# The sequential scan of a state-space layer: three operations a step on all groups in place of six on halves

## The chip, the cores and the metric

The kernel runs on one core of a Trainium2 chip. The metric is the device time of one execution in microseconds (us). Before the change it is 1076.48 us, the median of three runs between 1076.04 and 1077.04. One execution was also taken with the hardware profiler; it took 1074.8 us, and its instructions span 1073.0 us.

## The reference

One layer of a hybrid backbone on 1024 latent tokens of width 1024, with 256 context tokens ahead of them. What matters here is the S5 mixer: 64 groups of 16 channels, each with 64 complex states, scanned forwards and backwards.

```python
for d in range(2):                                   # forward, backward
    lb_re, lb_im, da_re, da_im, bb_re, bb_im = _s5_discretize(...)
    cu_re, cu_im = _apply_b(ucg, bb_re, bb_im)       # context tokens
    hc_re, hc_im = _diag_scan(cu_re, cu_im, da_re, da_im, rev)
    lu_re, lu_im = _apply_b(ug, bb_re, bb_im)        # latent tokens
    lu_re = lu_re.at[:, start].add(lb_re * h0_re - lb_im * h0_im)   # start from the context's last state
    lu_im = lu_im.at[:, start].add(lb_re * h0_im + lb_im * h0_re)
    h_re, h_im = _diag_scan(lu_re, lu_im, da_re, da_im, rev)        # h_t = lam_bar * h_(t-1) + bu_t
    y = y + _readout(h_re, h_im, c_re[d], c_im[d])
out = y + d_skip * u;  z = gelu(out);  y = z * sigmoid(z @ glu_w + glu_b)
x = x + g1 * y
x = x + g2 * mlp(modulate(rmsnorm(x)))               # squared ReLU, 1024 -> 4096 -> 1024
return rmsnorm(x)
```

## The kernel before

The state vector lies on the 128 partitions: 64 states forwards, 64 backwards. A column of the state tiles is one (group, real or imaginary part, time slot). Time is cut into chunks: 8 tokens make one local sum, computed by TensorE (`states`), and the recurrence runs over those chunks. It is done as a tree: `ups` (lines 501 to 509, with `step`, lines 468 to 477) combines the chunks pairwise twice, the **scan** (lines 684 to 714) goes through every fourth chunk in order, and `fill_fours` and `fill_pairs` (lines 675 and 737) go back down. What remains is the readout by TensorE, the gate and the MLP, whose large products are done by a seven-product block scheme and in three passes of rounded parts (`mm3`, line 782).

The scan has 39 steps, `q` = 1 to 39. Step `q` reads the state of slot `2q-1` and updates slot `2q+1`. `slot` (line 650) gives a view of 64 groups by 2 parts, 128 columns; its neighbouring columns are 28 words apart in the context tile `CT` and 132 words apart in the latent tile `LT`. The complex product needs four real products per group, and two additions collect them. Before the change, a step is six VectorE operations, two of each kind, on 32 groups each (`hf` = 0, 1):

- line 710 multiplies the 64 columns of a half of the old state, each used twice, by `L32`, the transition over 32 tokens, which lies in PSUM. It writes 128 columns to `m12[hf]` in PSUM (bank 1 for one half, bank 6 for the other).
- line 712 adds one half of these products, with the parts exchanged, to the new slot and writes 64 columns to `m3` in SBUF.
- line 714 adds the other products and `m3` and writes 64 columns to the new slot.

The order of work is written out by hand; every engine runs its own queue in program order, and a reader waits by semaphore for the writer, on the same engine too. Ahead of some steps stand other pieces: the finish of the kernels of a block of groups on VectorE (`k_finish`, lines 582 to 595, ahead of steps 9, 14, 20 and 28, each followed by eight stores on the SP queue), their products and copies on TensorE and ScalarE (steps 1, 6, 12, 20, 31), TensorE's conditioning products with their loads (line 406), two turns of a tile on ScalarE (line 668, at step 35) and, at step 34, a first part of `fill_fours` on GpSimd. After the last step come, on VectorE, `fill_fours` and `fill_pairs` of the first blocks (lines 473 to 476 are the four operations of `step`); GpSimd does those of one block; ScalarE copies each result (`hc_copy`, lines 734 and 735) for TensorE's readout (lines 763 and 764).

Of the kernel before, what the change touches and what calls it, by code (L numbers as in the profile page):

```python
# [10 lines left out]
OP = mybir.AluOpType  # L11
# [36 lines left out]
def kernel(ctx, tc, cst, bc, x, xl, ada_w, glu_w, w1, w2, out):  # L48
    nc = tc.nc
    V, S, P, PE, SP = nc.vector, nc.scalar, nc.gpsimd, nc.tensor, nc.sync  # L50
# [6 lines left out]
    UT = sp.tile([128, 2560], F32, name="UT")  # L57
# [4 lines left out]
    PS = pp.tile([128, 4096], F32, name="PS")  # L62
# [6 lines left out]
    def vw(ap, *dims):  # L69

        if len(dims) == 1:
            return ap
        names = "abcdef"[:len(dims)]
        return ap.rearrange("p (%s) -> p %s" % (" ".join(names), " ".join(names)),
                            **{names[i]: dims[i] for i in range(len(dims))})

    def size(dims):
        n = 1
        for d in dims:
            n *= d  # L80
        return n

    def at(tile_, off, *dims):
        return vw(tile_[:, off:off + size(dims)], *dims)
# [5 lines left out]
    def bank(i, n=512, o=0):  # L90
        return PS[:, 512 * i + o:512 * i + o + n]
# [86 lines left out]
    q = [at(UT, KT + 192 + 64 * i, 64) for i in range(6)]  # L178
# [56 lines left out]

    LR = [PS[:, o:o + 64] for o in (2048, 2240)]
    LI = [vw(PS[:, o + 64:o + 192], 64, 2) for o in (2048, 2240)]
    L32 = vw(PS[:, 2560:2816], 2, 32, 2, 2)
    TA, TB = 2432, 2960
    L32R, L32I = PS[:, 3840:3904], PS[:, 3904:3968]  # L240

# [21 lines left out]
        V.tensor_copy(L32I, pwi[:, :, 10])  # L263

    def scan_transitions():
        l32 = L32.rearrange("p a g k c -> p (a g) k c")
        V.tensor_copy(l32[:, :, 0], L32R[:, :, None].to_broadcast([128, 64, 2]))
        V.tensor_copy(l32[:, :, 1, 0], L32I)
        V.tensor_scalar(l32[:, :, 1, 1], L32I, -1.0, None, op0=OP.mult)
# [124 lines left out]
    def load_aw2(n, eng=SP):  # L394
        if n < 32:
            part, k = 2 + n // 8, n % 8
            eng.dma_start(out=aw2(n), in_=ada_w[128 * k:128 * k + 128, 1024 * part:1024 * part + 1024])

    def cond2_next():
        n = nc2[0]  # L400
        if n == 32:
            return
        nc2[0] += 1
        part, k = 2 + n // 8, n % 8
        for s in range(4):
            PE.matmul(bank(7)[32 * s:32 * s + 1, 0:256], sc[:, k, 0:1], aw2(n)[:, 256 * s:256 * s + 256], start=k == 0, stop=k == 7)
        late.extend([n + 2] if n + 2 <= C2C else [n + 2, n + 3] if n + 2 == C2C + 1 else [n + 3])
        if k < 7:
            return
        rw = sb(KS + 1024 * (part % 2), 1024)[0:1]  # L410
        for s in range(4):
            S.copy(rw[:, 256 * s:256 * s + 256], bank(7)[32 * s:32 * s + 1, 0:256])
        turns.append((part, rw))

    def cond2_turn():
        part, rw = turns.pop(0)
        for j in range(8):
            PE.transpose(bank(0)[:, 8 * part + j:8 * part + j + 1], rw[:, 128 * j:128 * j + 128], ident[0:1, 0:1])
# [60 lines left out]
    def woven(*streams):  # L479

        streams = [list(q) for q in streams]
        n = max(map(len, streams))
        for i in range(n):
            for q in streams:
                if i < len(q):
                    q[i]()
# [74 lines left out]
    def k_blocks(j):  # L561
        bd = sb(BD, 8, 2, 48)
        gs = slice(8 * j, 8 * j + 8)
        for c, b_ in ((0, br), (1, bi)):
            S.copy(bd[0:64, :, c, 32:48], b_[0:64, gs])
            S.copy(bd[64:128, :, c, 0:16], b_[64:128, gs])

    def k_mm(j, hlf):
        g8, bd, b = gt(j), sb(BD, 8, 2, 48), bank((2, 3)[hlf])
        for g in range(4):  # L570
            gg = 4 * hlf + g
            for c in range(2):
                PE.matmul(b[0:48, 128 * g:128 * g + 128], bd[:, gg, c], g8[:, gg, c], start=c == 0, stop=c == 1)  # L573

    def k_evac(j, hlf):
        bv = bank((2, 3)[hlf]).rearrange("p (g h t) -> p g t h", g=4, t=8)
        gh = slice(4 * hlf, 4 * hlf + 4)
        S.copy(ksr(j, 0, 8, 15, 16)[:, gh, 0:8], bv[0:16])
        S.copy(ksr(j, 0, 8, 15, 16)[:, gh, 8:15], bv[32:48, :, 1:8])
        S.copy(ksr(j, 1920, 8, 16)[:, gh], bv[32:48, :, 0])  # L580

    def k_finish(j, eng=V):

        k0, kf, dj = ksr(j, 0, 8, 15, 16)[:, :, 7], ksr(j, 1920, 8, 16), ksr(j, 2048, 8, 16)
        ks = kf
        if eng is V:
            r = 32 + 64 * (j % 2)
            dj, ks = (vw(PS[r:r + 16, o:o + 128], 8, 16) for o in (3200, 3328))
        eng.tensor_tensor(dj, ident[32:48, None, 32:48].to_broadcast([16, 8, 16]),
                        C("dg")[32:48, 8 * j:8 * j + 8, None].to_broadcast([16, 8, 16]), op=OP.mult)  # L590
        eng.tensor_tensor(ks, kf, dj, op=OP.add)
        eng.tensor_tensor(k0, k0, ks, op=OP.add)
        kd = KD[j].rearrange("(h t g c) -> t h g c", h=16, t=8, g=8)
        for t in range(8):
            SP.dma_start(out=kd[t], in_=ksr(j, 0, 8, 240)[:, :, 16 * (7 - t):16 * (7 - t) + 128])
# [48 lines left out]
    make_g(7)  # L644


    m3 = at(UT, 0, 2, 32, 2)
    m12 = [vw(bank(i, 128), 32, 2, 2) for i in (1, 6)]

    def slot(i):  # L650
        return CT[:, :, :, 0, i] if i < 14 else LT[:, :, :, 0, i - 14]
# [9 lines left out]
    def load_m8(j):  # L661
        SP.dma_start(out=at(X0, 1024 * (j % 2), 1024), in_=KD[j].rearrange("(p c) -> p c", p=128))

    def turn_m8(j):
        src = at(X0, 1024 * (j % 2), 8, 8, 16)
        dst = sb(M8 + 1024 * (j % 2), 8, 16, 8)
        if j <= POOL_FILL:
            S.copy(dst, src.rearrange("p g t h -> p g h t"))
        else:
            P.tensor_copy(dst, src.rearrange("p g t h -> p g h t"))  # L670

    def load_g0(k):
        SP.dma_start(out=at(X0, G0R, 2, 256), in_=glu_w.rearrange("(k p) n -> p k n", p=128)[:, k:k + 2, 0:256])

    def fill_fours(j, a=0, b=8, q0=0, q1=32, eng=None):

        eng = eng or (P if j == POOL_FILL else V)
        gs, n = slice(8 * j + a, 8 * j + b), q1 - q0
        x_ = LT[:, gs, :, 0]
        t = [at(GX, 0, b - a, 2, n)] * 2 if eng is P else [at(UT, 512 * i, b - a, 2, n) for i in range(2)]  # L680
        return step(x_[:, :, :, 2 * q0 + 2:2 * q1 + 1:2], x_[:, :, :, 2 * q0 + 1:2 * q1:2], 1, gs, *t, eng)

    scan_transitions()
    for q in range(1, 40):
        if q - 8 in KSTEP[:-1]:
            k_finish(3 + KSTEP.index(q - 8))
        if q in KSTEP:
            j = 3 + KSTEP.index(q)
            k_blocks(j)
            for hlf in range(2):  # L690
                k_mm(j, hlf)
                k_evac(j, hlf)
        if q % 3 == 0:
            cond2_next()
        while late:
            load_aw2(late.pop())
        if turns and q % 3 == 2:
            cond2_turn()
        if q == M8AT:
            turn_m8(0)  # L700
            turn_m8(1)
        if q == PRE + 7:
            woven(fill_fours(0, q1=PRE, eng=P))
        if q == 12:
            for i in range(2):
                load_m8(i)
            load_g0(0)
        for hf in range(2):
            p = slot(2 * q - 1)[:, 32 * hf:32 * hf + 32]
            V.tensor_tensor(m12[hf], p[:, :, None].to_broadcast([128, 32, 2, 2]), L32[:, hf], op=OP.mult)  # L710
        for hf in range(2):
            V.tensor_tensor(m3[:, hf], m12[hf][:, :, 1, ::-1], slot(2 * q + 1)[:, 32 * hf:32 * hf + 32], op=OP.add)
        for hf in range(2):
            V.tensor_tensor(slot(2 * q + 1)[:, 32 * hf:32 * hf + 32], m12[hf][:, :, 0], m3[:, hf], op=OP.add)
    while turns:
        cond2_turn()
    assert nc2[0] == 32
# [714 lines left out]
    for p in range(7, len(L)):  # L1432
        b, i = L[p]
# [80 lines left out]
    for d in range(8):  # L1514
        o = acc[:, d, toks[1]]
        S.activation(o, o, AF.Identity, scale=C("fg")[:, d:d + 1])
    rb = norm_rows(r_, 2, toks[1])
    for d in range(8):
        o = acc[:, d, toks[1]]
# [64 lines left out]
```

## Time and profile before

| | |
|---|---|
| median of the runs | 1076.48 us |
| profiled execution, whole | 1074.8 us |
| its span | 1073.0 us |
| PE busy | 954.5 us, 89% of the span |
| DVE busy | 884.0 us, 82% |
| ACT busy | 552.9 us, 52% |
| POOL busy | 599.7 us, 56% |
| the chain that ended last, by engine | PE 54%, DVE 24%, ACT 8%, issue 5%, POOL 4%, DMA 4% |

PE is TensorE, DVE is VectorE, ACT is ScalarE, POOL is GpSimd and SP is SyncE, which only issues transfers. A busy share over the whole span is an average over stages with different limits. The scan is one stage of about 50 us out of 1073.0, and what a change in it does is read from that stage and from what follows it.

### The profile page before, as it was taken

To read this page: it belongs to the slowest core of one execution; us is meant where nothing else is said; L and a number is where in the kernel's file an instruction comes from. 1 tells how busy PE (TensorE), PEld (TensorE's weight loads), DVE (VectorE), ACT (ScalarE), POOL (GpSimd) and SP (SyncE) were. 2 spreads that over 40 slices of the span, in tenths; PEclk is the share of its full clock that TensorE was granted. 3 is DMA by queue.
4 is the path that set the end of the run, shared out by engine and by line. 5 is a ranking of instruction groups with operands and counts; after the bars stand their busy time and mean duration, and the time that the engine had idled before them with its cause. 6 is when DMAs were issued, how large, how long until landed. Compare 5 with 4: busy or idle time off the path is not lost.

```text
span 1073.0 us, 15268 instructions
## 1 busy us (share of the span) xinstructions
PE 954.5 (89%) x5276; PEld 783.5 (73%) x5276; DVE 884.0 (82%) x1393; ACT 552.9 (52%) x1015; POOL 599.7 (56%) x411
## 2 busy tenths in 40 slices
PE   4788895656999998899999999998999999999995
PEld 4466674446888776588888888886678888888875
DVE  8799998999946776978665656656899999999997
ACT  6367683346973466656565554545444334343413
POOL 2868999735653814264232232324888787878603
PEclk9969797777999988999999999999999999999998
DMA  9514554775778211165545344469363535451204
GB/s 384 216 46 154 186 155 117 194 212 144 227 243 284 66 40 59 49 207 188 184 138 178 126 162 152 138 203 329 121 224 103 194 120 177 133 162 40 79 1 157
DMA packets 104782, 168.85 MB, mean 157 GB/s; under 512 B 7681, under 2 KB 61953, under 8 KB 103425
## 3 DMA queue, kind: packets, MB, share of 16 engines
q1 hardware_dynamic: 100272, 153.20, 43.6%
q10 hardware_dynamic: 4432, 14.68, 4.1%
q8 instruction: 41, 0.67, 0.3%
q14 instruction: 37, 0.29, 0.1%
HBM read 120.40 MB, written 47.45 MB: 156 GB/s over the span
## 4 chain that ended last, share of the span: by engine, by line
PE 54%; DVE 24%; ACT 8%; issue 5%; POOL 4%; DMA 4%; SPq 1%; DVEq 0%; ACTq 0%; POOLq 0%
PE PS L784 15%; PE PS L785 15%; PE PS L783 15%; DVE T L1364 3%; DVE X L476 2%; PE PS L154 2%; DVE X L475 2%; DMA DY<-X 1%; DVE z L934 1%; DVE PS L474 1%; DVE PS L473 1%; DVE W L934 1%; DVE PS L710 1%; PE PS L573 1%; PE PS L495 1%
## 5 line engine op out<-in xcount | busy, mean ns | idle before, releaser
L783 PE MATMUL PS<-z,W 128*128 128x512 f32 (+1 forms) x432 | 168.6, 390 | 2.9 <-DVE T L1184 1.5
L784 PE MATMUL PS<-z,W 128*128 128x512 f32 (+1 forms) x432 | 167.5, 388 | 2.5 <-DVE z L934 2.5
L785 PE MATMUL PS<-z,W 128*128 128x512 f32 (+1 forms) x404 | 156.7, 388 | 1.3 <-POOL W L934 1.2
L1364 DVE SCALAR_TENSOR_TENSOR T<-PS,T 128x512 f32<-128x512 f32 x160 | 112.1, 739 | 2.4 <-PE PS L785 2.2
L783 PEld LDWEIGHTS PS<-z,W 128*128 128x128 f32 x432 | 81.7, 189 | 21.2 <-DVE T L1463 2.2
L784 PE MATMUL PS<-W 128*128 128x512 f32 (+1 forms) x244 | 93.9, 385 | 3.4 <-DVE W L934 3.2
L784 PEld LDWEIGHTS PS<-z,W 128*128 128x128 f32 x432 | 81.7, 189 | 19.8 <-DVE z L934 3.7
L783 PE MATMUL PS<-W 128*128 128x512 f32 (+1 forms) x244 | 93.3, 382 | 0.0
L785 PEld LDWEIGHTS PS<-z,W 128*128 128x128 f32 x404 | 76.3, 189 | 17.9 <-POOL W L934 2.1
L934 DVE TENSOR_TENSOR z<-z 128x512 fp32r<-128x512 f32 x60 | 81.2, 1378 | 6.0 <-ACT z L937 6.0
L785 PE MATMUL PS<-W 128*128 128x512 f32 (+1 forms) x216 | 82.7, 383 | 1.5 <-POOL W L934 1.5
L785 PE MATMUL PS<-z,A 128*128 128x512 f32 x208 | 81.3, 391 | 2.5 <-POOL A L934 2.5
L934 DVE TENSOR_TENSOR W<-W 128x512 fp32r<-128x512 f32 x49 | 74.2, 1537 | 7.2 <-ACT W L937 7.2
L1212 POOL TENSOR_TENSOR T<-T 128x512 f32<-128x512 f32 x27 | 39.2, 1453 | 68.8 <-ACT T L1155 60.7
L785 PE MATMUL PS<-W,A 128*128 128x512 f32 x184 | 71.7, 390 | 0.3 <-POOL A L934 0.3
L783 PE MATMUL PS<-z,A 128*128 128x512 f32 x180 | 70.2, 390 | 0.0
L784 PE MATMUL PS<-z,A 128*128 128x512 f32 x180 | 70.0, 389 | 0.0
L1184 DVE TENSOR_TENSOR T<-T,PS 128x512 f32<-128x512 f32 x64 | 42.9, 685 | 32.4 <-PE PS L785 31.6
L937 ACT CAST W<-T 128x512 fp32r<-128x512 f32 (+1 forms) x46 | 33.0, 718 | 65.2 <-POOL T L1283 46.2
L937 ACT CAST W<-UT 128x512 fp32r<-128x512 f32 (+2 forms) x50 | 35.7, 714 | 58.6 <-POOL UT L1283 37.7
L495 PE MATMUL PS<-X,E 128*64 128x160 f32 x256 | 50.4, 339 | 14.5 <-DVE X L457 8.2
L783 PE MATMUL PS<-W,A 128*128 128x512 f32 x156 | 60.7, 389 | 0.0
(330 smaller groups left out, 2725.1 us busy)
## 6 DMA issues: line engine op xcount, KB each, us to landing
YD<-T SPq DMA_DIRECT2D x88, 256.0 KB, 2.3
z<-YD SPq DMA_DIRECT2D x60, 256.0 KB, 3.6
W<-YD SPq DMA_DIRECT2D x49, 256.0 KB, 4.2
T<-in_w_dram SPq DMA_DIRECT2D x9, 1024.0 KB, 5.8
T<-in_ada_w_dram ACTq DMA_DIRECT2D x17, 512.0 KB, 4.0
UT<-in_w_dram SPq DMA_DIRECT2D x8, 1024.0 KB, 5.9
T<-in_w_dram SPq DMA_DIRECT2D x20, 384.0 KB, 3.4
UT<-in_w_dram SPq DMA_DIRECT2D x15, 384.0 KB, 4.2
```

The source lines that it names most:

```text
L154: PE.matmul(ssq, C("sel"), a[:, g], start=(j, g) == (0, 0), stop=(j, g) == (7, 7))
L475: lambda: eng.tensor_tensor(out_, out_, ta, op=OP.add),
L476: lambda: eng.tensor_tensor(out_, out_, tb_, op=OP.add)]
L495: PE.matmul(b[0:64, c], e[:, g, c, 0:64], uj[:, g], start=True, stop=True)
L783: PE.matmul(o, wt[0], xt[0], start=start, stop=False)
L784: PE.matmul(o, wt[0], xt[1], start=False, stop=False)
L785: PE.matmul(o, wt[1], xt[0], start=False, stop=stop)
L934: eng.tensor_tensor(lo, src, hi.bitcast(F32), op=OP.subtract)
L937: S.copy(vw(to[0][:, 0:size(dims)], *dims) if dims else to[0], src)
L1184: V.tensor_tensor(to, x_, o, op=OP.add)
L1212: P.tensor_tensor(o, x_, z_, op=op)
L1364: V.scalar_tensor_tensor(o, src, g2[:, d:d + 1], o, op0=OP.mult, op1=OP.add)
```

## The change

The halves go. A step's product takes all 64 groups at once (256 columns), and so does each addition (128 columns). The product's target alternates from step to step between bank 1 and bank 6 of PSUM, where before each half had one of the two. `L32` and `m3` get the shapes for it.

```diff
-    L32 = vw(PS[:, 2560:2816], 2, 32, 2, 2)
+    L32 = vw(PS[:, 2560:2816], 64, 2, 2)
...
-        l32 = L32.rearrange("p a g k c -> p (a g) k c")
+        l32 = L32
...
-    m3 = at(UT, 0, 2, 32, 2)
-    m12 = [vw(bank(i, 128), 32, 2, 2) for i in (1, 6)]
+    m3 = at(UT, 0, 64, 2)
+    m12 = [vw(bank(i, 256), 64, 2, 2) for i in (1, 6)]
...
-        for hf in range(2):
-            p = slot(2 * q - 1)[:, 32 * hf:32 * hf + 32]
-            V.tensor_tensor(m12[hf], p[:, :, None].to_broadcast([128, 32, 2, 2]), L32[:, hf], op=OP.mult)
-        for hf in range(2):
-            V.tensor_tensor(m3[:, hf], m12[hf][:, :, 1, ::-1], slot(2 * q + 1)[:, 32 * hf:32 * hf + 32], op=OP.add)
-        for hf in range(2):
-            V.tensor_tensor(slot(2 * q + 1)[:, 32 * hf:32 * hf + 32], m12[hf][:, :, 0], m3[:, hf], op=OP.add)
+        p, o, m = slot(2 * q - 1), slot(2 * q + 1), m12[q % 2]
+        V.tensor_tensor(m, p[:, :, None].to_broadcast([128, 64, 2, 2]), L32, op=OP.mult)
+        V.tensor_tensor(m3, m[:, :, 1, ::-1], o, op=OP.add)
+        V.tensor_tensor(o, m[:, :, 0], m3, op=OP.add)
```

## Rows read from the trace of the kernel before

**Rows 1.** Windows: start:end, length, busy us (instructions) per engine, clock share, DMA.

```profile
core 0: us, PE busy (x) PEld busy (x) DVE busy (x) ACT busy (x) POOL busy (x), PEclk, DMA share, GB/s
186.50:237.10 50.60, 32.38 (x248) 23.09 (x248) 49.28 (x248) 15.89 (x41) 25.57 (x25) 0.74 0.75 193
...
254.00:264.00 10.00, 3.45 (x19) 3.26 (x18) 9.76 (x18) 9.76 (x14) 0.00 (x0) 0.67 0.40 120
```

**Rows 2.** Chain of waits around the scan's end: start us, us, what.

```profile
237.06 0.24 DVE UT L473
...
253.57 0.44 DVE X L476
...
254.03 0.05 ACT T L734
```

**Rows 3.** Timeline of DVE, one step and its neighbours: start us, us, operation, count.

```profile
229.09 0.56 DVE L710 TENSOR_TENSOR PS<-X,PS 128x128 f32<-128x128 f32 x2
229.56 0.43 DVE L712 TENSOR_TENSOR UT<-PS,X 128x64 f32<-128x64 f32 x2
229.90 0.40 DVE L714 TENSOR_TENSOR X<-PS,UT 128x64 f32<-128x64 f32 x2
230.20 0.56 DVE L710 TENSOR_TENSOR PS<-X,PS 128x128 f32<-128x128 f32 x2
```

**Rows 4.** Groups by line, DVE, in the scan: count, busy us, mean ns, idle before.

```profile
L710 DVE TENSOR_TENSOR PS<-X,PS 128x128 f32<-128x128 f32 x78 | 22.0, 327 | 0.2
L712 DVE TENSOR_TENSOR UT<-PS,X 128x64 f32<-128x64 f32 x78 | 16.8, 257 | 0.2
L714 DVE TENSOR_TENSOR X<-PS,UT 128x64 f32<-128x64 f32 x78 | 15.5, 265 | 0.0
L589 DVE TENSOR_TENSOR PS<-T 16x128 f32<-16x128 f32 x4 | 2.2, 561 | 0.1
L591 DVE TENSOR_TENSOR PS<-T,PS 16x128 f32<-16x128 f32 x4 | 1.2, 302 | 0.4
L592 DVE TENSOR_TENSOR T<-T,PS 16x128 f32<-16x128 f32 x4 | 1.1, 287 | 0.4
```

**Rows 5.** Timeline of DVE: the scan's first product, and a place of `k_finish`.

```profile
186.54 0.59 DVE L710 TENSOR_TENSOR PS<-X,PS 128x128 f32<-128x128 f32 x2
...
195.54 0.39 DVE L714 TENSOR_TENSOR X<-PS,UT 128x64 f32<-128x64 f32 x2
195.96 1.15 DVE L589 TENSOR_TENSOR PS<-T 16x128 f32<-16x128 f32 x1
```

**Rows 6.** Groups by line, DVE, from 80 to 186 us: products and sums elsewhere.

```profile
L474 DVE TENSOR_TENSOR PS<-X,PS 128x224 f32<-128x224 f32 x8 | 3.2, 397 | 0.3
L476 DVE TENSOR_TENSOR X<-X,PS 128x224 f32<-128x224 f32 x8 | 3.1, 389 | 0.3
L474 DVE TENSOR_TENSOR PS<-X,PS 128x112 f32<-128x112 f32 x8 | 2.2, 281 | 0.3
L476 DVE TENSOR_TENSOR X<-X,PS 128x112 f32<-128x112 f32 x8 | 2.2, 270 | 0.1
```

**Rows 7.** Waits from 186 to 240 us: who waited for whom, us, times, longest.

```profile
POOL GX L473 <- issue: 22.4, 1, 22.4
```

**Rows 8.** Waits from 237 to 310 us.

```profile
PEld PS L763 <- ACT T L735: 12.8, 7, 6.7
ACT T L734 <- DVE X L476: 7.9, 3, 2.8
```

**Rows 9.** Timeline of all engines behind the scan.

```profile
238.52 1.34 DVE L476 TENSOR_TENSOR X<-X,UT 128x80 f32<-128x80 f32 x1
...
241.08 0.62 ACT L734 COPY T<-X 64x512 f32<-64x512 f32 x1
```

**Rows 10.** Timeline of PE: one readout pair at either clock level.

```profile
247.06 0.63 PE L764 MATMUL PS<-T,E 128*128 128x128 f32 x2
...
251.88 0.39 PE L764 MATMUL PS<-T,E 128*128 128x128 f32 x2
```

## The prediction

> **What bounds the kernel now.** I read the busy time of the engines in the stretch of the scan first. From 186.5 to 237.1 us VectorE is busy 49.28 of 50.60 us, and every other engine far less, TensorE 32.38, GpSimd 25.57, ScalarE 15.89 [rows 1]. The scan is one long chain on one engine. Then the chain of waits, to see whether its end is also the end of something that counts: it goes from the scan straight into the fills on VectorE at 237.06 us, stays there until the fill that begins at 253.57 us, and goes on to ScalarE's copy at 254.03 us [rows 2]. Behind the scan nobody waits for a thing that the scan doesn't hold: ScalarE's copies wait 7.9 us for the fills, TensorE's readout 12.8 us for those copies [rows 8]. So a microsecond more or less in the scan moves what comes behind it.
>
> Last I read the timeline of one step. It begins at 229.09 us and the next at 230.20, so a step takes 1.11 us [rows 3], although its six operations last 2 x (327 + 257 + 265) = 1698 ns one by one [rows 4]. The difference is the thing to see. The second of a pair begins before the first has ended: the pair of products spans 0.56 us, so the second begins 0.56 - 0.327 = 0.233 us behind the first, 0.09 us ahead of its end. For line 712 it is 0.43 - 0.257 = 0.173 us, for line 714 0.40 - 0.265 = 0.135 us. Between kinds it is the same: line 712 begins at 229.56, when the pair of products ends only at 229.65. It can, because it reads the half that was finished first.
>
> Where an operation must read what the one just issued, or the one it waits for, has written, it begins about 0.03 us after that one's end: the product at 230.20 follows the first sum of line 714, which ends at 229.90 + 0.265 = 230.165 [rows 3, 4]; `k_finish` at 195.96 follows the last sum, which ends at 195.93 [rows 5].
>
> **What the change removes and adds.** It removes three of six operations a step, 117 in all, with their fixed parts. It also removes the second half, and with it all that a chain could overlap: the sum of line 712 reads the product just issued, the sum of line 714 reads that one's result, and the next product reads the slot just written. Three waits a step, each 0.035 us past an end, in place of one. The second bank buys nothing in this order: the next product waits for the slot anyway.
>
> The new durations are not in the trace; I work them out from products and sums of other sizes. A product costs 281 ns at 112 columns and 397 at 224, 1.036 ns a column; a sum 270 and 389, 1.06 ns a column [rows 6]. From these, a product of 128 columns would take 298, one of 256 430; a sum of 64 would take 219, one of 128 287. The scan's own take more: the product 327 - 298 = 29 ns, line 712 257 - 219 = 38, line 714 265 - 219 = 46 [rows 4, 6]. The scan differs in its columns, which lie 28 or 132 words apart.
>
> - Low end, if these extras are fixed per operation: 430 + 29 = 459, 287 + 38 = 325, 287 + 46 = 333, and three waits of 35: 1222 ns a step.
> - High end, if they grow with the columns: 430 + 58 = 488, 287 + 76 = 363, 287 + 92 = 379, and 105: 1335 ns.
>
> I take the high end. Lines 712 and 714 have the same 64 columns, but the pair of line 712, which reads spaced columns, is spaced by 0.173 us and that of line 714, which only writes them, by 0.135: 38 ns more, just its extra, so the extra occupies the stream and does not only lengthen the start.
>
> The page "Vector Engine (DVE) Microarchitecture Reference" of the Trainium skill, section "Measured stream behaviour on trn2", gives a hop at every element some 0.65 cycle a column, which at its 0.96 GHz is an estimate of 0.68 ns, or 43 for 64 columns. The trace's 38 and 46 for the sums agree; for the product the page would give 87 where the trace has 29. With the page's figure in the product, the step would be 116 ns longer and the total about 4.5 us above my forecast.
>
> Against that stands the scan as it is: from 186.54 [rows 5] to 237.06 us [rows 2] 50.5 us, of which the four places of `k_finish` are 2.2 + 1.2 + 1.1 busy and 0.9 idle, 5.4 [rows 4]. That leaves 45.1 us for 39 steps, 1.156 on average, more than 1.11 because of the steps in the context tile and the first step behind each break. After: 39 x 1.335 = 52.1 us, **7.0 us more**; at the low end 39 x 1.222 = 47.7, 2.6 more.
>
> **What lies beside it.** `k_finish` keeps its cost: its first operation writes PSUM columns that the wider product in bank 6 now covers too, but it starts 0.03 us behind the last sum already [rows 5]. Behind the new waits queue only the next operations of the chain; who waits for them has time: GpSimd's part of the fill sits idle 22.4 us before it begins [rows 7], and the stores of `k_finish` come up to 7 us later together with all that reads them. At the scan's end ScalarE is late by 241.08 - 239.86 = 1.2 us for its first copy [rows 9]; its turns and conditioning copies would be done earlier against the scan, but VectorE doesn't wait for that copy, so I count nothing.
>
> Sum against the profiled execution: 1074.8 + 7.0 = 1081.8 us, of which 1.8 lie around the span of 1073.0. The median of the runs is 1.7 us above that execution, so the forecast is 1076.5 + 7.0 = **1083.5 us**.
>
> **Rivals.**
>
> - *The extras are fixed.* Same mechanism, low end: +2.6, 1079.1 us. For it: the product's extra, with twice the columns, is smaller than those of the sums, not larger. Against: the spacing of line 712.
> - *Fewer operations win.* If a reader could start on the tail of its writer as the next of a pair does, a step would be three spacings at double size: 0.233 + 0.133 + 0.029 = 0.395, 0.173 + 0.068 + 0.038 = 0.279 and 0.135 + 0.068 = 0.203, together 0.877 us, 39 times 34.2: 10.9 us less, 1065.6 us. It decides in my disfavour if the gap from a writer's end to its reader's start is below about -0.02 us where it is +0.035 now (7.0 us over 117 gaps are 0.06 us). Against: the two places above, both at +0.03. The Trainium skill, "VectorE: DVE Perf Modes", section "Rules for kernel authors", says of chained operations "Minimize op *count*, not sems", since the pipe is emptied in any case; by that rule this rival would hold. The trace disagrees: the next of a pair starts 0.09 us before the end and a reader 0.03 after it.
> - *Part of it is hidden behind the scan.* If ScalarE and not VectorE set the pace from 241 us on, its 1.2 us of lateness are free: 1082.3. Against: ScalarE then waits 7.9 us for VectorE [rows 8].
> - *TensorE's clock falls otherwise.* Granted shares are 0.74 in the scan and 0.67 from 254 to 264 us [rows 1], a mixture of the levels 2.4 and 1.2 GHz; a pair of readout products takes 0.63 at the lower and 0.39 at the higher [rows 10], and a half block has eight such pairs, 8 x 0.24 = 1.9 us. A scan of other length can turn this either way: it widens the range by about 2 us.
>
> **How the numbers follow.** Forecast (extras grow) 0.67, with its own range 1081 to 1086; fixed extras 0.18; partly hidden 0.06; fewer operations win 0.05; otherwise 0.04. The range for 8 in 10 reaches down to the fixed extras and up by the clock: 1078.7 to 1086.5. What a measurement can tell from no change is 0.2%, 2.2 us, so up to 1078.6 counts as the same. Fixed extras at 1079.1 sit on that bound and lose a third of their chance to "same". Slower 0.87, same 0.07, faster 0.06.
>
> **What would show it.** In the changed kernel's trace, 39 operations of each kind instead of 78; products near 490 ns (460 if the extras are fixed), sums near 363 and 379 (325 and 333); every start 0.03 us after the end before it; a step of 1.335 us (1.222). The fills should begin some 7 us later, and the distance from there to the end should be the same. The prediction is wrong in its core if an operation begins before the one whose result it reads has ended, and in its second half if the fills begin 7 us later and the end doesn't.

## The result: 0.55% slower, and where the time went

The changed kernel takes 1082.27 us, the median of eight runs from 1079.83 to 1085.43; the kernel before took 1076.3 us on the same chip, eight runs from 1074.11 to 1080.29. The ratio is 1.0055 with a 95% interval of 1.0035 to 1.0075, that is +3.8 to +8.1 us. Forecast were +7.0 us and 1083.5; the range of 1078.7 to 1086.5 holds the time.

The profiled execution of the changed kernel spans 1078.1 us, 5.1 more than that of before. This is the same view as [rows 4], groups of VectorE by line in the scan; the last columns are busy us, mean ns of one, and the idle time before them. Line numbers are each kernel's own: here 709 is the product, 710 the sum into `m3`, 711 the sum into the slot.

```profile
L709 DVE TENSOR_TENSOR PS<-X,PS 128x256 f32<-128x256 f32 x39 | 19.7, 505 | 1.3
L711 DVE TENSOR_TENSOR X<-PS,UT 128x128 f32<-128x128 f32 x39 | 15.1, 388 | 1.3
L710 DVE TENSOR_TENSOR UT<-PS,X 128x128 f32<-128x128 f32 x39 | 14.8, 380 | 1.3
L589 DVE TENSOR_TENSOR PS<-T 16x128 f32<-16x128 f32 x4 | 1.9, 464 | 0.1
```

There are 39 of each kind in place of 78. VectorE's busy time for the three kinds falls from 22.0 + 16.8 + 15.5 = 54.3 us to 49.6, and yet the scan is longer: the busy times of before overlap, those of after don't. The idle columns say it too, 1.3 us ahead of each kind, 39 gaps of 0.034, where before they held 0.2, 0.2 and 0.0. The timeline of a step, start and duration in us, answers to [rows 3]:

```profile
230.02 0.50 DVE L709 TENSOR_TENSOR PS<-X,PS 128x256 f32<-128x256 f32 x1
230.55 0.38 DVE L710 TENSOR_TENSOR UT<-PS,X 128x128 f32<-128x128 f32 x1
230.97 0.38 DVE L711 TENSOR_TENSOR X<-PS,UT 128x128 f32<-128x128 f32 x1
231.38 0.50 DVE L709 TENSOR_TENSOR PS<-X,PS 128x256 f32<-128x256 f32 x1
```

Each start lies 0.03 to 0.04 us past the end ahead of it, and the step takes 1.36 us where it took 1.11. The mean durations above mix two tiles. In the latent tile (197 to 243.7 us, 31 steps), and for the product in the context tile (184.9 to 194.8 us, 7 steps), the same view gives:

```profile
L709 DVE TENSOR_TENSOR PS<-X,PS 128x256 f32<-128x256 f32 x31 | 15.5, 499 | 1.1
L711 DVE TENSOR_TENSOR X<-PS,UT 128x128 f32<-128x128 f32 x31 | 12.0, 387 | 1.1
L710 DVE TENSOR_TENSOR UT<-PS,X 128x128 f32<-128x128 f32 x31 | 11.7, 379 | 1.1
...
L709 DVE TENSOR_TENSOR PS<-X,PS 128x256 f32<-128x256 f32 x7 | 3.7, 532 | 0.2
```

The timeline at both ends of the scan gives its length, and behind it the first fills:

```profile
184.92 0.53 DVE L709 TENSOR_TENSOR PS<-X,PS 128x256 f32<-128x256 f32 x1
...
243.76 0.24 DVE L473 TENSOR_TENSOR UT<-X,PS 128x80 f32<-128x80 f32 x1
...
247.47 0.69 DVE L475 TENSOR_TENSOR X<-X,UT 128x512 f32<-128x512 f32 x1
```

From 184.92 to 243.76 us it is 58.8 us, against 50.5 before: 8.3 more. The rest of the account, by the offset between the two traces: the scan begins 1.6 us earlier, which is no effect of the change: the code ahead of it is the same, and the other runs below begin it anywhere from 1.8 us earlier to 1.5 later. (TensorE's granted clock over the first 80 us is 0.89 in the four traces that begin it 1.6 to 1.8 us earlier, this one among them, and 0.85 in all others.) Its end is 6.7 us later. At ScalarE's copy, which in [rows 2] begins at 254.03, it is 5.3 us; up to 400 us it stays between 5.1 and 5.8, and from there to the end it is 5.1 to 5.2:

```profile
258.91 0.44 DVE X L476
...
259.37 0.05 ACT T L731
```

So 1.4 us are given back in the fills right behind the scan. One operation shows most of it: the sum at 247.47 us takes 0.69 us, and its counterpart in the kernel before took 1.65. This is that one, with the first operation of GpSimd's fill and the one that runs beside it, in the timeline of the kernel before:

```profile
237.33 1.05 POOL L473 TENSOR_TENSOR GX<-X,T 128x512 f32<-128x512 f32 x1
...
240.97 1.30 POOL L476 TENSOR_TENSOR X<-X,GX 128x512 f32<-128x512 f32 x1
...
241.17 1.65 DVE L475 TENSOR_TENSOR X<-X,UT 128x512 f32<-128x512 f32 x1
```

and GpSimd's in the changed kernel:

```profile
241.08 0.45 POOL L592 TENSOR_TENSOR T<-T 16x128 f32<-16x128 f32 x1
242.50 1.05 POOL L473 TENSOR_TENSOR GX<-X,T 128x512 f32<-128x512 f32 x1 [0.96 <-DVE X L711]
...
246.13 1.30 POOL L476 TENSOR_TENSOR X<-X,GX 128x512 f32<-128x512 f32 x1
247.51 2.42 POOL L473 TENSOR_TENSOR GX<-X,T 128x1024 f32<-128x1024 f32 x1
```

In the kernel before GpSimd began its fill 0.27 us after VectorE's first fill (237.06), held by its own last piece of `k_finish`; here it is done with that 0.96 us before it can begin, waits for step 38 alone, and begins 1.26 us ahead of VectorE's first fill. So the two engines' operations meet otherwise. In the kernel before VectorE's sum starts 0.20 us into a GpSimd operation that ends at 242.27, and ends 0.55 us after that end; here it starts in the gap between two of them (247.43 to 247.51) and runs at its own length. In the traces of both kernels and of the runs below the fills' sums of 512 columns with both operands in SBUF behave alike up to 300 us: begun while a GpSimd operation runs, such a sum ends 0.54 to 0.57 us after that one's end; begun while none runs, it takes 0.68 to 0.72 us. One alone, begun 0.01 us after GpSimd's operation, took 0.68 us beside it.

### The profile page after: what moved, and what is told of

Same layout as the page of the kernel before. It is cut to its first block, busy times and chain, and to the rows that moved or that the text cites. A ratio compares the mean times of both kernels' runs of the same rounds, so it can differ in the third digit from the quotient of the medians.

```text
span 1078.1 us, 15151 instructions
## 1 busy us (share of the span) xinstructions
PE 950.9 (88%) x5276; PEld 781.4 (72%) x5276; DVE 887.3 (82%) x1276; ACT 552.7 (51%) x1015; POOL 598.2 (55%) x411
## 4 chain that ended last, share of the span: by engine, by line
PE 49%; DVE 26%; ACT 8%; DMA 7%; issue 5%; POOL 4%; SPq 1%; DVEq 0%; ACTq 0%; POOLq 0%
PE PS L781 14%; PE PS L782 14%; PE PS L780 14%; DVE T L1361 3%; DMA DY<-X 2%; DVE X L476 2%; PE PS L154 2%; DVE X L475 2%; DVE z L931 1%; DVE PS L709 1%; DVE PS L474 1%; DVE PS L473 1%; DVE W L931 1%; DMA T<-DY 1%; DVE X L711 1%
```

## The experiments

The theory to test: the change pays for waiting. A reader starts 0.035 us past its writer's end; with two halves the engine filled that time with the other half. The rivals: an operation's fixed cost is paid whole in any case and the wide operations are dear by themselves; the extra time of the scan's operations is fixed or comes from something else than the spacing of the columns; part of the added time comes from other waits.

**One bank for the products.** One part of the change undone.

```diff
-        p, o, m = slot(2 * q - 1), slot(2 * q + 1), m12[q % 2]
+        p, o, m = slot(2 * q - 1), slot(2 * q + 1), m12[0]
```

> The changed kernel with one part of it undone: the products of all steps go to one bank. Theory 1: the next product waits for the slot, which is written after the bank's last read has been issued, so nothing changes: step 1.376 us, total 6 us above the kernel before (+4 to +8). Rival (the second bank saves a wait for the readers of the products): the step is longer by 0.03 us or more, the total 1 us or more above the changed kernel.

The ratio is 1.0072 (1.0053 to 1.0091), overlapping that of the changed kernel. In the groups of the scan the durations are the same, and so are the idle times:

```profile
L709 DVE TENSOR_TENSOR PS<-X,PS 128x256 f32<-128x256 f32 x39 | 19.7, 505 | 1.3
L711 DVE TENSOR_TENSOR X<-PS,UT 128x128 f32<-128x128 f32 x39 | 15.1, 388 | 1.3
L710 DVE TENSOR_TENSOR UT<-PS,X 128x128 f32<-128x128 f32 x39 | 14.7, 378 | 1.3
```

The scan takes 58.7 us. The second bank neither costs nor saves. Until 450 us this run's trace lies 5.5 us behind that of the kernel before, much as the changed kernel's does; 2.5 us more come on TensorE between 450 and 480 us, where its granted clock over 440 to 470 us is 0.83 in this trace (first row) and 0.94 in the changed kernel's (second row; columns as in [rows 1]):

```profile
440.00:470.00 30.00, 26.78 (x95) 20.13 (x94) 26.62 (x39) 15.94 (x26) 12.17 (x9) 0.83 0.27 93
...
440.00:470.00 30.00, 26.62 (x107) 20.28 (x106) 25.88 (x37) 15.01 (x25) 12.42 (x10) 0.94 0.28 97
```

**No reader right behind its writer.** First try, in all steps:

```diff
-        p, o, m = slot(2 * q - 1), slot(2 * q + 1), m12[q % 2]
+        m, n, k, k_ = m12[q % 3], m12[(q - 1) % 3 if q > 1 else 1], m3[q % 3], m3[(q - 1) % 3 if q > 1 else 1]
+        p, o, o_ = slot(max(2 * q - 5, 1)), slot(2 * q + 1), slot(2 * q - 1)
...
-        V.tensor_tensor(m3, m[:, :, 1, ::-1], o, op=OP.add)
-        V.tensor_tensor(o, m[:, :, 0], m3, op=OP.add)
+        V.tensor_tensor(k, n[:, :, 1, ::-1], o, op=OP.add)
+        V.tensor_tensor(o_, n[:, :, 0], k_, op=OP.add)
```

> The changed kernel's three whole operations a step, but each reads what was written a step earlier (product of the state two steps back, sums of the previous step's products), so none reads what the one just ahead of it wrote; the recurrence is not computed. The count, widths and memories of the operations are as in the changed kernel. Theory 1 (a reader starts 0.035 us past its writer's end, while an operation that reads older data starts some 0.1 us ahead of the end in front of it): starts move 0.09 to 0.13 us ahead of ends, a step falls from 1.38 to 0.88 to 0.96 us, the scan by 16 to 19 us against the changed kernel, the total to 1064 to 1069, below the kernel before. Rival (an operation's fixed cost is paid whole in any case, and wide operations on spaced columns are dear by themselves): the step stays at 1.27 to 1.38 us and the total at 1078 to 1083.

The total missed: ratio 1.0089 (1.0064 to 1.0114), 1085.8 us. The edit had brought two waits of its own, which the list of waits of VectorE in that stretch shows:

```profile
DVE PS L710 <- DMA X<-in_ada_w_dram: 9.8, 1, 9.8
DVE X L712 <- POOL GX L474: 2.6, 1, 2.6
```

The product of step 9 now read a context slot whose place a load had meanwhile taken, and the late sums met GpSimd's fill. Two of the three product areas shared a bank, and the steps in which one operation wrote one area of that bank and a neighbour read the other kept a wait of 0.034 us past the end, though the columns are not the same (1.04 to 1.15 us in all); the third kind of step took 0.90 to 0.95. So a shared bank alone is enough for a wait here. As a test of the total it settles nothing. The second try keeps to steps 10 to 32 and puts the areas in three banks:

```diff
+        late_ = 10 <= q <= 32
+        i, i_ = q % 3, (q - (q > 10 and late_)) % 3
+        p, o, o_ = slot(2 * q - (5 if late_ else 1)), slot(2 * q + 1), slot(2 * q + (-1 if late_ else 1))
+        V.tensor_tensor(m12[i], p[:, :, None].to_broadcast([128, 64, 2, 2]), L32, op=OP.mult)
+        V.tensor_tensor(m3[i], m12[i_][:, :, 1, ::-1], o, op=OP.add)
+        V.tensor_tensor(o_, m12[i_][:, :, 0], m3[i_], op=OP.add)
```

> The changed kernel where in steps 10 to 32 each operation reads what was written a step earlier (the recurrence is not computed there), with three product areas in three PSUM banks, so that no operation touches the bank of the one ahead of it, and with the finish of block 6 ahead of step 34. Theory 1 (waiting for the writer's end is what the change pays): each start lies 0.09 to 0.17 us ahead of the end in front of it, every step of these takes 0.90 to 0.95 us in place of 1.37, though the durations stay at 498, 377 and 387 ns; the scan takes 47 to 48.5 us; the total is 1071 to 1075. Rival (fixed costs are paid whole in any case): the step stays at 1.27 or more, the total at 1082.

Ratio 0.9991 (0.9975 to 1.0007), 1074.55 us. The timeline of a step:

```profile
216.57 0.52 DVE L712 TENSOR_TENSOR PS<-X,PS 128x256 f32<-128x256 f32 x1
216.99 0.39 DVE L713 TENSOR_TENSOR UT<-PS,X 128x128 f32<-128x128 f32 x1
217.27 0.42 DVE L714 TENSOR_TENSOR X<-PS,UT 128x128 f32<-128x128 f32 x1
217.49 0.54 DVE L712 TENSOR_TENSOR PS<-X,PS 128x256 f32<-128x256 f32 x1
```

The step takes 0.92 us with the same three operations at the same widths, each starting 0.10 to 0.20 us ahead of the end in front of it. From step 11 on, but for the steps on either side of a `k_finish`, it is 0.89 to 0.92. The durations did not fall; the product's are 0.49 to 0.56 us, the sums' 0.36 to 0.44. Of the 1.36 us of a step, then, some 0.45 are the price of waiting: 0.10 in three gaps, the rest in overlap that a waiting operation can't have. The scan takes 49.5 us. This run also gives every operation another bank than its neighbour's, but the bank can't be the whole cause of the waits: in the changed kernel the product writes another bank than the sum ahead of it reads, and it waits 0.034 us like the others, for the slot in SBUF. Without the wait, three operations do beat six: 0.92 against the 1.11 of the kernel before. The first rival falls.

**Packed columns, three operations.** The states of 19 steps lie in a packed tile, filled and emptied by ScalarE.

```diff
+    def state(q):
+        return at(UT, 128 + 128 * (q - QA), 64, 2) if QA <= q <= QB else slot(2 * q + 1)    # QA, QB = 8, 26
+    def packed(a, b):
+        d = at(UT, 128 + 128 * (a - QA), b - a, 64, 2).rearrange("p n g c -> p g c n")
+        return d, LT[:, :, :, 0, 2 * a - 13:2 * b - 14:2]
...
-        p, o, m = slot(2 * q - 1), slot(2 * q + 1), m12[q % 2]
+        p, o, m = state(q - 1), state(q), m12[q % 2]
```

> The changed kernel, with the states of steps 8 to 26 in a packed SBUF tile (neighbouring columns adjacent): ScalarE packs the slots ahead of step 8 and puts them back after steps 17 and 26. Three operations a step as in the changed kernel. Theory 1 (the extra time of the scan's operations comes from columns that lie 132 words apart and grows with their number): in the packed steps the product falls from 498 to 435 to 445 ns, the sums from 377 and 387 to 287 to 300, a step from 1.376 to about 1.13 us, the scan by 4.6 us; the total is 1 to 2.5 us above the kernel before in place of 6. Rival (the extra comes from the repeated and reversed patterns or from waiting, not from the spacing): durations and step stay, the total is 6 us above the kernel before.

The timeline of a packed step:

```profile
217.89 0.43 DVE L725 TENSOR_TENSOR PS<-UT,PS 128x256 f32<-128x256 f32 x1
218.36 0.29 DVE L726 TENSOR_TENSOR UT<-PS,UT 128x128 f32<-128x128 f32 x1
218.68 0.29 DVE L727 TENSOR_TENSOR UT<-PS,UT 128x128 f32<-128x128 f32 x1
219.01 0.43 DVE L725 TENSOR_TENSOR PS<-UT,PS 128x256 f32<-128x256 f32 x1
```

Product 429 ns, sums 290 and 291, step 1.11 us, scan 54.3 us, 4.5 less than in the changed kernel: close to what was expected, the product and the step a little lower. So the spacing of the columns is what makes the scan's operations dear: against 499, 379 and 387 ns in the latent tile it costs 70, 89 and 96 ns for 256, 128 and 128 columns. The total, expected 1 to 2.5 us above the kernel before, missed: ratio 1.0052 (1.0033 to 1.0071). In its one trace the lag behind the kernel before is 3.0 us from 250 to 370 us, as the scan would have it, and 4.6 on TensorE from 460 us on, where its granted clock came to the higher of its two levels at 463 us (438 in the kernel before). Whether the median, 5.6 us above the kernel before, lost its 3 us in the same place I can't tell from one trace.

**Packed columns, six operations.** The same on the kernel before.

```diff
-            p = slot(2 * q - 1)[:, 32 * hf:32 * hf + 32]
+            p = state(q - 1)[:, 32 * hf:32 * hf + 32]
```

> The kernel before with six operations a step on halves, and the states of steps 8 to 26 packed in the same way. Theory 1 (the halves are spaced by the engine's stream, whose share for spaced columns goes): spacings fall to 0.20 (products), 0.135 (both sums), a step from 1.11 to 0.94 to 1.0 us, the scan by 2 to 3.2 us, the total to 1073 to 1074.5, unless ScalarE's copies delay the finish of the kernels ahead of step 9. Rival (extra not from spacing): step 1.11, total as before or 0.5 above it for ScalarE's copies.

The packed steps take 0.92 us, and the total doesn't move: ratio 0.9997 (0.9984 to 1.0011), scan 50.5 us. The timeline of VectorE shows where the gain went:

```profile
215.02 0.48 DVE L726 TENSOR_TENSOR PS<-UT,PS 128x128 f32<-128x128 f32 x2
...
216.19 0.29 DVE L589 TENSOR_TENSOR PS<-T 16x128 f32<-16x128 f32 x1
221.12 0.29 DVE L591 TENSOR_TENSOR PS<-T,PS 16x128 f32<-16x128 f32 x1 [4.63 <-ACT T L580]
```

Ahead of step 28 `k_finish` waits 4.63 us for ScalarE's copy (line 580) of TensorE's products of block 6; without this wait the scan would take 45.9 us. In the kernel before that copy ended at 220.23 us, 2.06 us ahead of `k_finish`; here it ends at 221.08, and the scan has overtaken it. Some of the wait is of the packing's own making: ScalarE's copy back ahead of step 18 (2.44 us from 210.68) stands ahead of that block's preparation, and TensorE's products for it begin at 213.78 us where they began at 212.68, though this scan started 1.6 us earlier.

**GpSimd's fill ahead of its last finish.** Is what was given back behind the scan really GpSimd's pairing? On the kernel before:

```diff
-    k_finish(7, P)
     load_u(1)
     load_m8(3)
     woven(fill_fours(POOL_FILL))
     woven(fill_pairs(POOL_FILL))
+    k_finish(7, P)
```

In this and the two runs that follow, `load_u(1)` writes over a part of block 7's kernel that is not finished yet, so that part of the readout is not the reference's.

> The kernel before with one piece moved on GpSimd: the finish of the last block of kernels comes behind its two fills instead of ahead of them. Theory 1 (of the changed kernel's longer scan some 1 us is given back behind it, because GpSimd, held there by that finish until 237.3 us in the kernel before, starts its fill when the last but one step is done, and two VectorE sums then run beside another operation of GpSimd): here GpSimd's fill starts near 235.9 us in place of 237.3, the VectorE sum at 241.2 takes 0.7 in place of 1.65 us, the fills up to 250 us are 0.9 to 1.4 us shorter, the total 0.5 to 1.4 us less, 1074 to 1075. Rival (what was given back comes from ScalarE's earlier copies): nothing moves, the total stays at 1075.3.

GpSimd's and VectorE's timelines:

```profile
235.92 1.05 POOL L473 TENSOR_TENSOR GX<-X,T 128x512 f32<-128x512 f32 x1 [1.25 <-issue]
```

```profile
240.89 0.68 DVE L475 TENSOR_TENSOR X<-X,UT 128x512 f32<-128x512 f32 x1
```

The pairing does it: GpSimd starts 1.4 us earlier, the sum falls in the gap between two of its operations (240.86 to 240.94) and takes 0.68 us, and VectorE is 1.2 us ahead at 250 us, with the scan unchanged. The total does not show it: ratio 1.0007 (0.9992 to 1.0021). In the trace the lead is 2.5 us at 450 us and, on TensorE, gone at 480; its granted clock came to the higher level at 459 us (438 in the kernel before).

**Six packed operations, reordered.** The finish of block 6 later, GpSimd's as above, one copy back; and its control without packing.

```diff
+KFIN = (9, 14, 20, 34)
...
-        if q - 8 in KSTEP[:-1]:
-            k_finish(3 + KSTEP.index(q - 8))
+        if q in KFIN:
+            k_finish(3 + KFIN.index(q))
```

> Six operations a step with the packed states of steps 8 to 26, as in the packed-six run, but the finish of block 6 is ahead of step 34 instead of 28, GpSimd's last finish is behind its fills, and ScalarE puts all 19 states back in one copy at step 27. Theory 1 (there the shorter steps were lost in a wait of 4.6 us for ScalarE's copies of block 6, which TensorE and the loads pace and not the scan): no wait over 0.5 us in the scan, step 0.92 us where packed, scan near 47 us, the total 2 to 4.5 us less than the kernel before, 1071 to 1073.5. Rival (something else that the scan doesn't pace is late next, such as ScalarE's copy at 241 us): scan near 47 us, but the fills or their copies wait, and the total stays within 1 us of the kernel before.

> The kernel before with the two moves of order alone (finish of block 6 ahead of step 34, GpSimd's last finish behind its fills), without packing. Theory 1: as with the second move alone, 0.5 to 1.4 us less than the kernel before; the first move costs nothing. It is the measure for the run with packing. Rival: the later finish of block 6 makes its stores late for their reader and costs 1 us or more.

With packing 1072.46 us, ratio 0.9967 (0.9953 to 0.9982), scan 46.8 us and no wait of VectorE in it; without, 1077.64 us, 1.0015 (1.0001 to 1.003). The moves alone gain nothing, against what I expected: the interval is a loss of 0.1 to 3.2 us, so the rival, a cost of 1 us or more, is not ruled out. With them the packing shows in the time.

**The version that does the whole computation.** GpSimd's finish stands between its two fills, ahead of `load_u(1)`:

```diff
+    woven(fill_fours(POOL_FILL))
     k_finish(7, P)
     load_u(1)
     load_m8(3)
-    woven(fill_fours(POOL_FILL))
     woven(fill_pairs(POOL_FILL))
```

> The reordered kernel with six operations a step and packed states again, but GpSimd's finish of the last block stands between its two fills, ahead of the load that goes to the same place in SBUF; the whole computation is done. Theory 1: the steps and the scan are as in the reordered run (0.92 us where packed, scan near 47 us), GpSimd's second fill is 1.3 us later, and the total is 3 to 4 us less than the kernel before: 1072 to 1073.5. Rival (the later second fill of GpSimd, or ScalarE's copies, is late for the readout of block 2): scan near 47 us, but the total within 1 us of the kernel before.

1072.14 us, ratio **0.9962** (0.9946 to 0.9978), 4.1 us less than the kernel before (3 to 4 were expected). A packed step, and the end of the scan:

```profile
214.23 0.48 DVE L727 TENSOR_TENSOR PS<-UT,PS 128x128 f32<-128x128 f32 x2
214.62 0.35 DVE L729 TENSOR_TENSOR UT<-PS,UT 128x64 f32<-128x64 f32 x2
214.89 0.34 DVE L731 TENSOR_TENSOR UT<-PS,UT 128x64 f32<-128x64 f32 x2
215.15 0.48 DVE L727 TENSOR_TENSOR PS<-UT,PS 128x128 f32<-128x128 f32 x2
...
232.02 0.24 DVE L474 TENSOR_TENSOR UT<-X,PS 128x80 f32<-128x80 f32 x1
```

The scan begins at 186.19 and takes 45.8 us. The groups of the packed steps (196.5 to 216 us) give the halves without spacing:

```profile
L727 DVE TENSOR_TENSOR PS<-UT,PS 128x128 f32<-128x128 f32 x36 | 8.7, 288 | 0.1
L729 DVE TENSOR_TENSOR UT<-PS,UT 128x64 f32<-128x64 f32 x36 | 6.3, 217 | 0.1
L731 DVE TENSOR_TENSOR UT<-PS,UT 128x64 f32<-128x64 f32 x36 | 6.2, 215 | 0.0
```

Spaced, in the latent tile of the kernel before (199 to 236.9 us), they take 324, 257 and 265 ns, so the spacing costs 36, 40 and 50 ns at half the columns.

## Why the prediction was right, point by point

- *Three waits a step in place of one, and no overlap left.* Right, and shown: each of the scan's 117 operations starts 0.031 to 0.035 us past the end of the one ahead of it, and the run without readers behind their writers brings the step from 1.36 to 0.92 us at the same widths. The rule "Minimize op *count*, not sems" of the Trainium skill ("VectorE: DVE Perf Modes", "Rules for kernel authors"), given there for chained operations, would have had the change gain. These traces disagree: in a chain three operations take 1.36 us and six on two halves 1.11; only where no operation waits for its neighbour do three take 0.92.
- *The extras grow with the columns.* Right, shown by the packed runs: 36, 40 and 50 ns at half the columns, 70, 89 and 96 at all of them. The argument from the spacing of the pairs was weaker than its conclusion. Packed, the second of the pair of line 712 follows the first at 0.135 us in place of 0.17, as it said; for line 714 it is 0.130 in place of 0.135, nearly no change, and its extra grew with the columns all the same. The sizes were a little low: product 499 ns in the latent tile where 488 were forecast, sums 379 and 387 where 363 and 379. The step came to 1.376 us on average for 1.335, 39 steps to 53.7 us for 52.1. The mis-sized terms are the extras taken from lines 474 and 476, 29, 38 and 46 where the packed halves give 36, 40 and 50; doubled, that is 26 of the 41 ns. Another 8 or so are the seven steps in the context tile, which take 1.41 us and had no term of their own.
- *`k_finish` keeps its cost.* Nearly: 5.2 us for 5.4.
- *Nothing beside the scan hides a part.* This failed: the distance from the fills' start to the end, which should have stayed, fell by 1.4 us up to 254 us and by 1.6 to the end. I looked for cover on ScalarE and priced it at nothing; 1.4 us came back through GpSimd, which in the kernel before was held by its own last finish. The row read for GpSimd, in [rows 7], is the idle time ahead of its part at step 34 (230.30 us), not ahead of its fill at 237.33. The two errors, 1.6 us too little in the steps and 1.4 too much behind them, nearly cancel, and that is luck. By the medians the change costs 5.9 us where 7.0 were forecast, and the interval of 3.8 to 8.1 can't tell the two apart.
- *The second bank buys nothing.* Right: one bank gives the same durations and gaps.
- *TensorE's clock as a width of 2 us.* Right in size: 1.5 to 2.6 us. It showed at other places than I named: at 450 to 480 us, and ahead of the scan. The traces of the kernel before and of the changed one are alike at 450 to 480 us, so the difference between these two owes nothing to it there.

## What to carry to other kernels

In a chain on one engine, count for each operation what it waits for before counting operations: merging two independent halves saves their fixed parts and turns them into waits for the writer's end, here 0.45 us of a 1.36 us step. On packed columns the order is the same, 1.11 us for three operations and 0.92 for six. Two independent streams in turn are worth keeping until the engine itself is the limit, as in the kernel before; then the cost of an operation is what is left to cut, and here it was the spacing of its columns. When a stage is made faster, look for the next thing that it overtakes: in the first packed run of six the whole gain was lost in one wait of 4.63 us for a copy that had been on time before.

## What the hardware showed that I had not expected

- Columns that lie 132 words apart cost 89 ns for 128 columns read by a sum and 96 when a sum writes them, 0.70 and 0.75 ns a column; a product that reads 128 spaced columns twice each pays 70 ns for its 256, 0.27 ns a column. The Trainium skill ("Vector Engine (DVE) Microarchitecture Reference", "Measured stream behaviour on trn2") has some 0.65 cycle for a hop at each element, by its 0.96 GHz an estimate of 0.68 ns: the sums agree, the product pays less than half of it. In the context tile, where the columns lie 28 words apart, the product takes 532 ns, 33 more than at 132 words.
- A VectorE sum with both operands in SBUF takes 0.68 us or, behind the scan of the kernel before, 1.65 to 2.29 us at the same 512 columns: begun while a GpSimd operation runs, it ends 0.55 us after that one's end, so its length is what is left of that operation and 0.55 us. A shift of 1.4 us in GpSimd's start is worth 1 us on VectorE.
- Runs of one kernel spread over 6 us (1073.0 to 1079.6 us in 35 runs of the kernel before). In the traces, TensorE's granted clock at 440 to 470 us differs between kernels whose code there is the same: it comes to the higher of its two levels at 434 to 444 us in five of them and at 459 to 470 in the other six, and those lose 1.5 to 2.6 us there against the kernel before. What sets it is open. It is a likely reason, not shown, why a difference of 1 us in the fills could be seen in a trace and not in the medians.
